# Score products that contract over their own 32 or 64 rows, in a two-block transformer kernel on one core

## The chip, the core and the metric

The kernel runs on one core of a Trainium2 chip. Five engines of the core work side by side, each through its own list of instructions in order: PE (TensorE, matrix products into PSUM banks), DVE (VectorE), ACT (ScalarE), POOL (GpSimd) and SP, which only issues DMAs. They wait for each other through semaphores. The metric is the device time of one execution in microseconds (us), the median of several runs.

A matmul loads a stationary operand (PEld in the profile) and streams the other through an array of 128 rows (the contraction) by 128 columns. A matmul whose operands occupy 32 or 64 partitions uses only that group of the array's rows; such a part is called a tile of the array below, written rows x columns (32x128, 64x128).

## What is computed

Two transformer blocks follow each other, each with two layers, on 256 tokens of width 1024. The first block mixes tokens with three branches (latent attention, differential attention, pooling), the second with sliding-window attention, an mLSTM and an RWKV-7 recurrence. Cut to the products that matter here:

```
# differential attention, 8 heads, two maps m of 32 channels each
sc = einsum('bqhmd,bkhmd->bmhqk', q, k) * scale - slopes * dist
a  = softmax(sc)[:, 0] - lam * softmax(sc)[:, 1]
# sliding-window attention, 8 query heads on 2 key heads of 64 channels
scores = einsum('bnqhgd,bnkhd->bnhgqk', qb, kb) * HEAD_DIM ** -0.5
# mLSTM, 4 heads of 64 channels
s = einsum('bhcld,bhcsd->bhcls', q, k) * w_intra
# RWKV-7, 4 heads of 64 channels, in the kernel's chunked form:
# products of (b, k) with (a, r) over the 64 channels of a head
```

## The kernel before

Activations lie transposed, channels on the 128 partitions and 256 tokens along the free dimension, so one 128-partition slab holds four 32-channel maps or two 64-channel heads. Large products run as fp32r pairs: each weight tile is split into a high part (`wh`, ACT, L444) and a low part (`wl`, DVE, L445), and `mm3` (L329) issues three fp32r matmuls per tile. The score products, transposes and recurrences are plain fp32, and each plain fp32 matmul appears in the trace as two MATMUL rows of its size, two passes.

In the plain form a score product contracts over all 128 partitions. To get one head out of the slab, one operand is first multiplied with a 0/1 column (`m4` or `m2`) that clears the other heads' rows:

- differential attention (`diff` in `_mix_a`, L1047 to L1055): four masked copies `qm` of the query slab on DVE for each slab and query half `qt`; for each head two matmuls (maps m = 0, 1) into one bank `S`; one DVE instruction adds the distance term for both maps. The score is 256 keys wide for `qt` = 1 and 128 for `qt` = 0.
- RWKV (`rwkv`, L1230 to L1278): two masked copies `BKm` of `BK` (DVE and ACT); for each of eight units (half `h`, slab `j`, head `e`) two 256-wide matmuls into one bank `rw`, then a DVE mask.
- mLSTM (`mlstm`, L1464 to L1493): two masked query copies on ACT; for each head a 256-wide and a 128-wide matmul into `S`.
- sliding window (`swa`, L1559 to L1579): two masked key copies on DVE; for each of four query slabs and each `qt` two matmuls into one bank `S`.

PSUM banks come from pools with a fixed number of buffers: `mm` 2 (also used by the projections), `S` 2 in the first block's mixer and 1 in the second's, `rw` 2, `PT` and `O`. The mixers are generators whose parts are written alternately with the projections of `gemm` (in the second block RWKV alternates with mLSTM and then the window attention). The final order on each engine is chosen by the framework's list scheduler when the kernel is built; only instructions passed to `chain` or `behind` are held in place. None of the score products is.

Of the kernel before, what the change touches and what calls it, by code (L numbers as in the profile page):

```python
# [13 lines left out]
AF = mybir.ActivationFunctionType  # L14
ALU = mybir.AluOpType
# [3 lines left out]
P = 128  # L19
T = 256  # L20
# [5 lines left out]
NEG = -1e30  # L26
# [186 lines left out]
def two(b):  # L213
    return b.rearrange("p (a t) -> p a t", a=2)
# [6 lines left out]
def bc(x, n):  # L221

    return x.unsqueeze(1).to_broadcast([x.shape[0], n, x.shape[1]])
# [641 lines left out]
def _mix_a(s, nrm, l, nxt, ws, ahead):  # L865
    nc, A = s.nc, s.A
# [21 lines left out]
    rq, _ = s.rstd(s.colsum(sq1), 2, 256 / 96, 96 * EPS)  # L888
    sq2 = s.tile([P, T], "row")
    nc.scalar.activation(sq2, ckv, AF.Square)  # L890
    rk, _ = s.rstd(s.colsum(sq2), 2, P)
# [3 lines left out]
    for j in range(2):  # L895
        b = s.gemm([A["a_win"][l, 7]], act)[0] if j else bp
# [6 lines left out]
    for c in range(3):  # L903
        b = s.ps("S")
# [28 lines left out]
    for c in range(2):  # L933
        b = s.ps("S")
# [8 lines left out]
    for h in range(2):  # L943
        b = s.ps("S")
# [10 lines left out]
    for st in range(4):  # L955
# [4 lines left out]
        m = s.tile([P, T], "row")  # L960
# [5 lines left out]
    for c in range(2):  # L966
        b = s.ps("S")
        for j in range(2):
            g = 2 * c + j
            s.mm3(b[:, j * T:(j + 1) * T], wp, g * P, P, pq[g], j == 0, True)  # L970
        for j in range(2):
            g = 2 * c + j
            y = s.tile([P, T], "row")
            nc.vector.tensor_scalar(y, b[:, j * T:(j + 1) * T], s.v(f"a_pb_{l}", g), s.v(f"a_ps_{l}", g),
                                    op0=ALU.add, op1=ALU.mult)
            s.split(yp[g][:, 0], yp[g][:, 1], y)

    dqk = Wide(s, 8, "cc")
# [61 lines left out]
    def diff(qt):  # L1040
        nk = P * (qt + 1)
        ob = s.ps("O")
        dm = s.dist[:, 0:256] if qt else s.dist[:, 256:384]
        for j in range(4):
            qm = s.tile([P, 4, P], "qm")
            for i in range(4):
                nc.vector.tensor_scalar(qm[:, i], dqk[j][:, qt * P:(qt + 1) * P], s.c("m4", i, i + 1), None, op0=ALU.mult)  # L1047
            for e in range(2):
                hd = 2 * j + e
                b = s.ps("S")  # L1050
                for m in range(2):
                    nc.tensor.matmul(b[:, m * nk:(m + 1) * nk], lhsT=qm[:, 2 * e + m], rhs=dqk[4 + j][:, :nk],
                                     start=True, stop=True)
                sc = s.tile([P, 2, nk], "sc")
                nc.vector.scalar_tensor_tensor(sc, bc(dm, 2), -(2.0 ** -(hd + 1)), two(b[:, :2 * nk]), op0=ALU.mult, op1=ALU.add)  # L1055
                rs = softmax_rows(s, sc)
# [7 lines left out]
                if hd == 7:  # L1064
# [12 lines left out]
                    for i in range(2):  # L1077
                        hi, lo = yd.pair(i)
# [62 lines left out]
def rwkv(s, nrm, l, rb, first, wrk, yh, yl):  # L1141
# [87 lines left out]
    nc.vector.tensor_tensor(BK[:, 1], k2, Ei, op=ALU.mult)  # L1229
    BKm = [s.tile([P, 2, 2, T], "ra") for _ in range(2)]  # L1230
    nc.vector.tensor_scalar(BKm[0], BK, s.c("m2", 0, 1), None, op0=ALU.mult)
    nc.scalar.activation(BKm[1], BK, AF.Copy, scale=s.c("m2", 1, 2))
    shift(0, b0)
# [33 lines left out]
    un = []  # L1267
    for h in range(2):
        for j in range(2):
            for e in range(2):  # L1270
                u = 4 * h + 2 * j + e
                b = s.ps("rw")
                rhs = AR[:, 2 * j + h].rearrange("p a t -> p (a t)")
                nc.tensor.matmul(b[:, 0:T], lhsT=BKm[e][:, 1, j, hs(h)], rhs=rhs, start=True, stop=True)
                nc.tensor.matmul(b[:, T:], lhsT=BKm[e][:, 0, j, hs(h)], rhs=rhs, start=True, stop=True)
                if u % 2 == 0:
                    un.append(s.tile([P, 2, 512], "ra"))
                nc.vector.tensor_tensor(un[u // 2][:, u % 2], b, s.m("mk4"), op=ALU.mult)  # L1278
            yield
# [136 lines left out]
def mlstm(s, nrm, l, rb, wif, yh, yl):  # L1416
# [32 lines left out]
    for c in range(2):  # L1449
# [13 lines left out]
        yield  # L1463
    qm = s.tile([P, 2, 2, T], "att")  # L1464
    for e in range(2):
        nc.scalar.activation(qm[:, e], qk[:, 0:2], AF.Copy, scale=s.c("m2", e, e + 1))
    va = s.tile([P, 2, 4, 65], "va")
# [13 lines left out]
    for hd in range(4):  # L1481
        j, e = hd // 2, hd % 2
        bm = s.ps("PT")
        nc.tensor.matmul(bm[:, :T], lhsT=s.c("ident")[:4, hd:hd + 1].to_broadcast([4, P]), rhs=M[:4], start=True, stop=True)
# [4 lines left out]
        nc.scalar.activation(wm[:, T:], wm[:, T:], AF.Exp, bias=cm[:, 4 + hd:5 + hd])  # L1489
        b = s.ps("S")  # L1490
        nc.tensor.matmul(b[:, :T], lhsT=qk[:, 2 + j, :P], rhs=qm[:, e, j], start=True, stop=True)
        nc.tensor.matmul(b[:, T:T + P], lhsT=qk[:, 2 + j, P:], rhs=qm[:, e, j, P:], start=True, stop=True)
        nc.vector.scalar_tensor_tensor(wm, b[:, :384], 1.0 / 32, wm, op0=ALU.mult, op1=ALU.mult)  # L1493
        if e == 0:
# [39 lines left out]
def swa(s, nrm, l, rb, yh, yl):  # L1534
# [23 lines left out]
    rope(kv[:, 0:1], 1)  # L1558
    km = s.t2("km")  # L1559
    for e in range(2):  # L1560
        nc.vector.tensor_scalar(km[:, e], kv[:, 0], s.c("m2", e, e + 1), None, op0=ALU.mult)
    yield
# [6 lines left out]
    for qt in (1, 0):  # L1569
        nk = P * (qt + 1)  # L1570
        ob = s.ps("O")
        for i in range(4):
            b = s.ps("S")
            for e in range(2):
                nc.tensor.matmul(b[:, e * nk:(e + 1) * nk], lhsT=q[:, i, qt * P:(qt + 1) * P], rhs=km[:, e, :nk],  # L1575
                                 start=True, stop=True)
            sc = s.tile([P, 2, nk], "sc")
            nc.vector.scalar_tensor_tensor(sc, bc(s.m("sw", 0 if qt else P, 256), 2), NEG, two(b[:, :2 * nk]),
                                           op0=ALU.mult, op1=ALU.add)  # L1579
            mx, sm, es, rs = (s.tile([P, 2], "t8") for _ in range(4))  # L1580
# [214 lines left out]
```

## Time and profile before

| | |
|---|---|
| median of 3 runs | 2460.52 us (2458.12 to 2463.18) |
| profiled execution: its time, its span | 2463.42 us, 2461.6 us |
| PE busy | 2400.8 us (98% of the span) |
| DVE, ACT, POOL busy | 1854.3, 1476.0, 43.6 us |
| mean granted TensorE clock | 0.992 of full |

The mixers of the first block lie at about 241 to 395 and 846 to 1000 us, those of the second at 1447 to 1600 and 2061 to 2215 us; the rest are feed-forward stages. A matmul's duration in the trace is a modelled latency that overlaps its neighbours', so what a matmul costs PE is read from the distance between starts, not from its duration.

### The profile page before, as it was taken

The numbers are of one execution on the slowest core, as the hardware profiler recorded it, in microseconds if no ns is written. First come the engines' busy times: TensorE is split into PE (matmuls) and PEld (weight loads), VectorE is DVE, ScalarE is ACT, GpSimd is POOL, SyncE is SP. The second block draws the span as 40 slices with busy tenths as digits, with TensorE's granted clock in tenths as the row PEclk, the third lists the DMA queues.
The fourth block names the chain that finished last, engine by engine and source line by source line (L and its number), as shares of the span: only waits on it lengthen the run. The fifth ranks groups of instructions, "written<-read, shape, count | busy, mean of one in ns | idle before, by whom it ended". The sixth has DMA issues, their size and how long they took to land. (4 is left out here: it accounts for less than half of the span.)

```text
span 2461.6 us, 45601 instructions
## 1 busy us (share of the span) xinstructions
PE 2400.8 (98%) x17164; PEld 2232.8 (91%) x17164; DVE 1854.3 (75%) x3620; ACT 1476.0 (60%) x2954; POOL 43.6 (2%) x43
## 2 busy tenths in 40 slices
PE   8999999999999999999999999999989999999998
PEld 6999999999899999999999888989989998898997
DVE  7667988767766888877786688777767678877765
ACT  6556765656655676566565564466666566346664
POOL 0000000000000000000000000000000000000000
PEclk9999999999999999999999999999999999999998
DMA  6554445555555444555555532146535553215651
GB/s 223 185 188 156 146 138 171 189 189 189 176 191 193 136 148 146 172 194 187 185 182 187 189 131 86 35 170 208 194 110 178 189 189 131 86 35 172 211 197 60
DMA packets 110510, 396.62 MB, mean 161 GB/s; under 512 B 12752, under 2 KB 13264, under 8 KB 110288
## 3 DMA queue, kind: packets, MB, share of 16 engines
q1 hardware_dynamic: 109008, 391.33, 47.5%
q8 instruction: 135, 2.21, 0.4%
q10 hardware_dynamic: 1280, 2.36, 0.3%
q14 instruction: 87, 0.71, 0.1%
HBM read 392.60 MB, written 1.05 MB: 160 GB/s over the span
## 5 line engine op out<-in xcount | busy, mean ns | idle before, releaser
L445 DVE TENSOR_TENSOR wl<-raw,wh 128x512 fp32r<-128x512 f32 (+1 forms) x1446 | 980.4, 686 | 266.8 <-ACT wh L444 246.9
L444 ACT ACTIVATE wh<-raw 128x512 fp32r<-128x512 f32 (+1 forms) x1446 | 895.7, 628 | 472.9 <-PE mm L329 118.4
L336 PE MATMUL mm<-act,wh 128*128 128x512 f32 x1728 | 614.0, 395 | 13.0 <-ACT wh L444 8.9
L337 PE MATMUL mm<-act,wl 128*128 128x256 f32 x1728 | 482.8, 280 | 0.7 <-DVE wl L445 0.7
L329 PE MATMUL acc<-h,wh 128*128 128x256 f32 x2560 | 457.0, 280 | 0.0
L329 PE MATMUL mm<-act,wh 128*128 128x256 f32 (+1 forms) x2176 | 420.7, 289 | 9.5 <-ACT act L447 3.4
L336 PEld LDWEIGHTS mm<-act,wh 128*128 128x128 f32 x1728 | 324.5, 188 | 85.4 <-ACT wh L444 9.1
L329 PEld LDWEIGHTS acc<-h,wh 128*128 128x128 f32 x2560 | 391.2, 188 | 4.0 <-ACT h L444 0.3
L329 PEld LDWEIGHTS mm<-act,wh 128*128 128x128 f32 (+1 forms) x2176 | 341.5, 190 | 15.8 <-ACT act L447 4.5
L329 PE MATMUL acc<-h,wl 128*128 128x256 f32 x1280 | 355.7, 279 | 0.0
L337 PEld LDWEIGHTS mm<-act,wl 128*128 128x128 f32 x1728 | 326.8, 189 | 1.8 <-DVE wl L445 1.2
L329 PE MATMUL mm<-act,wl 128*128 128x256 f32 x1088 | 310.8, 287 | 0.0
L336 PE MATMUL up<-act,wh 128*128 128x512 f32 x832 | 296.4, 394 | 0.1
L329 PEld LDWEIGHTS acc<-h,wl 128*128 128x128 f32 x1280 | 240.5, 188 | 0.3
L337 PE MATMUL up<-act,wl 128*128 128x256 f32 x832 | 232.6, 280 | 0.0
L329 PEld LDWEIGHTS mm<-act,wl 128*128 128x128 f32 x1088 | 206.4, 190 | 2.6 <-issue 1.8
L336 PEld LDWEIGHTS up<-act,wh 128*128 128x128 f32 x832 | 156.3, 188 | 34.3 <-DVE uu L344 0.5
L337 PEld LDWEIGHTS up<-act,wl 128*128 128x128 f32 x832 | 157.3, 189 | 0.4
L343 ACT ACTIVATE jn<-mm 128x256 f32<-128x256 f32 x216 | 80.1, 371 | 83.7 <-PE mm L337 83.6
L728 ACT ACTIVATE ga<-ga 128x512 f32<-128x512 f32 x88 | 55.1, 630 | 93.5 <-DVE ga L727 93.4
L344 DVE TENSOR_TENSOR ga<-mm,jn 128x256 f32<-128x256 f32 x112 | 46.9, 419 | 64.7 <-ACT jn L343 64.7
L336 PE MATMUL acc<-act,wh 128*128 128x512 f32 x256 | 92.9, 401 | 1.4 <-ACT wh L444 1.4
(506 smaller groups left out, 3233.7 us busy)
## 6 DMA issues: line engine op xcount, KB each, us to landing
raw<-a_wgate SPq DMA_DIRECT2D x88, 512.0 KB, 4.5
raw<-a_wup SPq DMA_DIRECT2D x88, 512.0 KB, 4.1
raw<-a_wdown SPq DMA_DIRECT2D x88, 512.0 KB, 4.3
raw<-b_wgate SPq DMA_DIRECT2D x88, 512.0 KB, 4.5
raw<-b_wup SPq DMA_DIRECT2D x88, 512.0 KB, 4.3
raw<-b_wdown SPq DMA_DIRECT2D x88, 512.0 KB, 4.5
raw<-a_win SPq DMA_DIRECT2D x80, 512.0 KB, 3.7
raw<-a_wbr SPq DMA_DIRECT2D x24, 512.0 KB, 3.7
```

The source lines that it names most:

```text
L329: pin(s.nc.tensor.matmul(out, lhsT=w[x], rhs=a[:, y], start=start and i == 0, stop=stop and i == 2, skip_group_check=True))
L336: s.nc.tensor.matmul(bank, lhsT=hi, rhs=a.rearrange("p a t -> p (a t)"), start=start, stop=False, skip_group_check=True)
L337: s.nc.tensor.matmul(bank[:, :T], lhsT=lo, rhs=a[:, 0], start=False, stop=stop, skip_group_check=True)
L343: s.nc.scalar.activation(t, b[:, T:], AF.Copy)
L344: s.nc.vector.tensor_tensor(out[:, i], b[:, :T], t, op=ALU.add)
L444: pin(nc.scalar.activation(hi, src, AF.Copy))
L445: pin(nc.vector.tensor_tensor(lo, src, hi.bitcast(F32), op=ALU.subtract))
L728: nc.scalar.activation(ga, ga, AF.Silu)
```

## The change

The masked copies go. Each score matmul takes as operands only the partitions of its own head (32 in `diff`, 64 elsewhere), and the matmuls of different row groups write different PSUM banks. The instruction that consumed one bank with both maps becomes two, one for each bank (`diff`, `swa`). In `rwkv` two banks are taken per (h, j), in `mlstm` both heads of a slab are computed at once into one bank of `S` and one of `mm`, and in `swa` likewise `S` and `mm`. The window keys are copied once by ACT where DVE wrote two masked copies.

```diff
         for j in range(4):
-            qm = s.tile([P, 4, P], "qm")
-            for i in range(4):
-                nc.vector.tensor_scalar(qm[:, i], dqk[j][:, qt * P:(qt + 1) * P], s.c("m4", i, i + 1), None, op0=ALU.mult)
             for e in range(2):
                 hd = 2 * j + e
-                b = s.ps("S")
+                sc = s.tile([P, 2, nk], "sc")
+                bm = [s.ps("S")[:, :nk] for _ in range(2)]
                 for m in range(2):
-                    nc.tensor.matmul(b[:, m * nk:(m + 1) * nk], lhsT=qm[:, 2 * e + m], rhs=dqk[4 + j][:, :nk],
-                                     start=True, stop=True)
-                sc = s.tile([P, 2, nk], "sc")
-                nc.vector.scalar_tensor_tensor(sc, bc(dm, 2), -(2.0 ** -(hd + 1)), two(b[:, :2 * nk]), op0=ALU.mult, op1=ALU.add)
+                    g = slice((2 * e + m) * 32, (2 * e + m) * 32 + 32)
+                    nc.tensor.matmul(bm[m], lhsT=dqk[j][g, qt * P:(qt + 1) * P], rhs=dqk[4 + j][g, :nk], start=True, stop=True)
+                for m in range(2):
+                    nc.vector.scalar_tensor_tensor(sc[:, m], dm, -(2.0 ** -(hd + 1)), bm[m], op0=ALU.mult, op1=ALU.add)
...
-    BKm = [s.tile([P, 2, 2, T], "ra") for _ in range(2)]
-    nc.vector.tensor_scalar(BKm[0], BK, s.c("m2", 0, 1), None, op0=ALU.mult)
-    nc.scalar.activation(BKm[1], BK, AF.Copy, scale=s.c("m2", 1, 2))
...
         for j in range(2):
+            bs = [s.ps("rw"), s.ps("rw")]
+            for i in range(2):
+                for e in range(2):
+                    g = slice(e * 64, e * 64 + 64)
+                    nc.tensor.matmul(bs[e][:, i * T:(i + 1) * T], lhsT=BK[g, 1 - i, j, hs(h)],
+                                     rhs=AR[g, 2 * j + h].rearrange("p a t -> p (a t)"), start=True, stop=True)
+            un.append(s.tile([P, 2, 512], "ra"))
             for e in range(2):
...
-                nc.vector.tensor_tensor(un[u // 2][:, u % 2], b, s.m("mk4"), op=ALU.mult)
+                nc.vector.tensor_tensor(un[-1][:, e], bs[e], s.m("mk4"), op=ALU.mult)
...
-    qm = s.tile([P, 2, 2, T], "att")
-    for e in range(2):
-        nc.scalar.activation(qm[:, e], qk[:, 0:2], AF.Copy, scale=s.c("m2", e, e + 1))
...
         j, e = hd // 2, hd % 2
+        if e == 0:
+            bs = [s.ps("S"), s.ps("mm")]
+            for lo, hi, k in ((0, T, 0), (T, 384, P)):
+                for i in range(2):
+                    g = slice(i * 64, i * 64 + 64)
+                    nc.tensor.matmul(bs[i][:, lo:hi], lhsT=qk[g, 2 + j, k:k + P], rhs=qk[g, j, k:], start=True, stop=True)
...
-    km = s.t2("km")
-    for e in range(2):
-        nc.vector.tensor_scalar(km[:, e], kv[:, 0], s.c("m2", e, e + 1), None, op0=ALU.mult)
+    km = s.tile([P, T], "km")
+    nc.scalar.activation(km, kv[:, 0], AF.Copy)
...
-            b = s.ps("S")
+            bs = [s.ps("S")[:, :nk], s.ps("mm")[:, :nk]]
             for e in range(2):
-                nc.tensor.matmul(b[:, e * nk:(e + 1) * nk], lhsT=q[:, i, qt * P:(qt + 1) * P], rhs=km[:, e, :nk],
-                                 start=True, stop=True)
+                g = slice(e * 64, e * 64 + 64)
+                nc.tensor.matmul(bs[e], lhsT=q[g, i, qt * P:(qt + 1) * P], rhs=km[g, :nk], start=True, stop=True)
```

What this does to the order on PE, at three places. First the differential attention, first layer, `qt` = 1: a row gives the line, the operation, the output tile, the operands and the output's size. Before, at the two heads of one slab:

```order
L329 MATMUL mm_805_3774<-act_532_2420,wl_804_3771 128x256
L1052 MATMUL S_808_3831<-cc_677_3206,qm_807_3826 128x256 x2
L1052 MATMUL S_815_3853<-cc_677_3206,qm_807_3826 128x256 x2
L329 MATMUL mm_832_3895<-act_527_2376,wh_824_3879 128x256 x2
L329 MATMUL mm_832_3895<-act_527_2376,wl_825_3880 128x256
```

And after, at one head of the same attention:

```order
L1051 MATMUL S_844_3969<-cc_677_3206,cc_639_3014 128x256
L329 MATMUL mm_861_4012<-act_527_2376,wl_856_4001 128x256
L329 MATMUL mm_861_4012<-act_527_2376,wh_855_4000 128x256 x2
L329 MATMUL mm_861_4012<-act_527_2376,wl_856_4001 128x256
L1060 MATMUL O_779_3704<-cc_704_3331,pT_815_3845 128x64 x2
L1051 MATMUL S_845_3970<-cc_677_3206,cc_639_3014 128x256
L329 MATMUL mm_861_4012<-act_532_2420,wh_857_4004 128x256 x2
```

The two maps of a head, which stood in one run of four, now stand apart, with full 128-row matmuls between them.

Second, the stretch in the second block where the RWKV scores (`rw`) and the mLSTM scores (`S`, `mm`) are made, first layer. Before (L1274 and L1275 are RWKV, L1491 and L1492 mLSTM, L329 a projection):

```order
L1274 MATMUL rw_3902_18657<-rp_3863_18468,ra_3865_18474 128x256
L1275 MATMUL rw_3902_18657<-rp_3863_18468,ra_3865_18474 128x256
L329 MATMUL mm_3964_18887<-act_3770_17900,wh_3960_18879 128x256 x2
L1491 MATMUL S_3908_18674<-att_3871_18493,att_3814_18199 128x256
L1492 MATMUL S_3908_18674<-att_3871_18493,att_3814_18199 128x128
L329 MATMUL mm_3964_18887<-act_3770_17900,wl_3961_18880 128x256
```

After (L1269 is RWKV, L1480 mLSTM, L1482 spreads one row of 4 over the partitions, L1492 is the product with the values):

```order
L1269 MATMUL rw_3915_18634<-rp_3879_18452,ra_3880_18453 128x256 x2
L1482 MATMUL PT_3927_18671<-row_3820_18144,cst_4_63 128x256
L1480 MATMUL S_3919_18644<-att_3830_18183 128x256
L1480 MATMUL mm_3920_18645<-att_3830_18183 128x256
L1480 MATMUL S_3919_18644<-att_3830_18183 128x128
L1480 MATMUL mm_3920_18645<-att_3830_18183 128x128
L1480 MATMUL mm_3933_18693<-att_3830_18183 128x256
L1480 MATMUL mm_3933_18693<-att_3830_18183 128x128
L1269 MATMUL rw_3916_18635<-rp_3879_18452,ra_3880_18453 128x256 x2
L1482 MATMUL PT_3934_18698<-row_3820_18144,cst_4_63 128x256
L1269 MATMUL rw_3924_18662<-rp_3879_18452,ra_3880_18453 128x256 x2
L1492 MATMUL O_3923_18658<-va_3885_18473,sc_3922_18652 128x65
```

The RWKV scores now come bank by bank, both matmuls of a bank (one row group) together, and the projection's rows between them have moved behind this stretch.

Third, the window attention of the same layer, after (L1570 is the score product, `S` for the lower and `mm` for the upper 64 rows; L1308 and L1313 belong to RWKV); before, each slab's two matmuls stood as one row with x2:

```order
L1570 MATMUL mm_4034_19188<-km_3983_18926,att_3986_18940 128x256
L1299 MATMUL rw_3985_18934<-ra_3945_18744,ra_3931_18689 128x128 x2
L1299 MATMUL rw_3985_18934<-ra_3945_18744,ra_3939_18716 128x128 x2
L1308 MATMUL rw_4000_19017<-ra_3946_18745,ra_3944_18743 128x128 x4
L1570 MATMUL S_4033_19187<-km_3983_18926,att_3986_18940 128x256
L1313 MATMUL rw_4001_19023<-ra_3944_18743,ra_3946_18745 128x128 x4
L1570 MATMUL mm_4045_19233<-km_3983_18926,att_3986_18940 128x256
L1570 MATMUL mm_4058_19290<-km_3983_18926,att_3986_18940 128x256
```

Here too the two row groups of a slab are separated by full matmuls, and two matmuls of the same row group can stand together.

## Rows read from the trace of the kernel before

**Rows 1.** The page, part 1: busy us of each engine (share of span).

```profile
PE 2400.8 (98%) x17164; PEld 2232.8 (91%) x17164; DVE 1854.3 (75%) x3620; ACT 1476.0 (60%) x2954; POOL 43.6 (2%) x43
```

**Rows 2.** Stretches: window, length, busy us of PE, PEld, DVE, ACT, POOL; clock, DMA.

```profile
241.00:395.00 154.00, 154.00 (x1259) 149.20 (x1258) 134.16 (x330) 102.94 (x250) 3.81 (x2) 1.00 0.46 147
1447.00:1600.00 153.00, 148.63 (x1153) 137.59 (x1152) 121.04 (x293) 70.71 (x160) 7.37 (x4) 0.99 0.21 72
```

**Rows 3.** Waits of PE, 1447 to 1600 us: total us, times, longest.

```profile
PE mm L372 <- DVE sc L1452: 1.2, 1, 1.2
PE rw L1217 <- DVE ud L1212: 1.2, 1, 1.2
PE mm L329 <- ACT va L1471: 1.0, 1, 1.0
PE PT L1443 <- DVE row L1437: 0.5, 1, 0.5
PE mm L329 <- DVE att L1566: 0.3, 1, 0.3
```

**Rows 4.** Groups by form, score matmuls: busy us, mean ns, idle before.

```profile
L1052 PE MATMUL S<-cc,qm 128*128 128x256 f32 x64 | 15.6, 382 | 0.0
L1274 PE MATMUL rw<-rp,ra 128*128 128x256 f32 x32 | 9.5, 379 | 0.0
L1575 PE MATMUL S<-km,att 128*128 128x256 f32 x32 | 8.2, 380 | 0.0
L1491 PE MATMUL S<-att,att 128*128 128x256 f32 x16 | 5.1, 399 | 0.0
```

**Rows 5.** Timeline of PE: start us, us, engine, line; 128-row tiles.

```profile
1539.25 1.03 PE L1575 MATMUL S<-km,att 128*128 128x256 f32 x4
1540.12 1.05 PE L1318 MATMUL rw<-ra,ra 128*128 128x128 f32 x8
1541.01 0.64 PE L1304 MATMUL rw<-ra,ra 128*128 128x128 f32 x4
```

**Rows 6.** Timeline of PE: a 64-row tile between 128-row tiles.

```profile
1526.00 0.94 PE L1304 MATMUL rw<-ra,ra 128*128 128x128 f32 x7
1526.87 0.71 PE L1388 MATMUL st<-rp,rp 64*128 64x128 f32 x4
1527.51 1.16 PE L1313 MATMUL rw<-ra,ra 128*128 128x128 f32 x8
1528.51 0.38 PE L1544 MATMUL PT<-sc,cst 128*128 128x256 f32 x1
```

**Rows 7.** Timeline of PE: a 4-row matmul (32-row tile) between projections.

```profile
1496.83 0.40 PE L329 MATMUL mm<-act,wh 128*128 128x256 f32 x2
1497.07 0.28 PE L329 MATMUL mm<-act,wl 128*128 128x256 f32 x1
1497.28 0.69 PE L1484 MATMUL PT<-row,cst 4*128 4x256 f32 x2
1497.90 0.50 PE L329 MATMUL mm<-act,wh 128*128 128x256 f32 x2
1498.24 0.28 PE L329 MATMUL mm<-act,wl 128*128 128x256 f32 x1
```

**Rows 8.** Timeline of PE: matmuls alternating between two 64-column tiles.

```profile
1564.34 1.09 PE L1333 MATMUL rw<-ra,rp 128*64 128x128 f32 x16
1565.37 0.49 PE L1575 MATMUL S<-km,att 128*128 128x128 f32 x2
```

**Rows 9.** Groups by form on DVE: busy us, mean ns, idle before.

```profile
L1047 DVE TENSOR_SCALAR qm<-cc,cst 128x128 f32<-128x128 f32 x64 | 14.0, 279 | 0.0
L1055 DVE SCALAR_TENSOR_TENSOR sc<-dist,S 128x512 f32<-128x512 f32 x16 | 10.9, 680 | 1.2 <-PE PT L844 0.9 <-PE S L1052 0.4
L1055 DVE SCALAR_TENSOR_TENSOR sc<-dist,S 128x256 f32<-128x256 f32 x16 | 6.6, 414 | 0.9 <-PE S L1052 0.7
L1231 DVE TENSOR_SCALAR ra<-ra,cst 128x1024 f32<-128x1024 f32 x2 | 1.5, 745 | 0.0
```

More of the change, by code (lines that the diff above doesn't have):

```diff
@@ L1269, in rwkv @@
         for j in range(2):
-            for e in range(2):
[L1271 to L1277, printed above, removed]
-                nc.vector.tensor_tensor(un[u // 2][:, u % 2], b, s.m("mk4"), op=ALU.mult)
+            bs = [s.ps("rw"), s.ps("rw")]
[5 more added lines that the diff above has]
+            un.append(s.tile([P, 2, 512], "ra"))
+            for e in range(2):
+                nc.vector.tensor_tensor(un[-1][:, e], bs[e], s.m("mk4"), op=ALU.mult)
             yield
@@ L1489, in mlstm @@
         nc.scalar.activation(wm[:, T:], wm[:, T:], AF.Exp, bias=cm[:, 4 + hd:5 + hd])
-        b = s.ps("S")
-        nc.tensor.matmul(b[:, :T], lhsT=qk[:, 2 + j, :P], rhs=qm[:, e, j], start=True, stop=True)
-        nc.tensor.matmul(b[:, T:T + P], lhsT=qk[:, 2 + j, P:], rhs=qm[:, e, j, P:], start=True, stop=True)
-        nc.vector.scalar_tensor_tensor(wm, b[:, :384], 1.0 / 32, wm, op0=ALU.mult, op1=ALU.mult)
+        nc.vector.scalar_tensor_tensor(wm, bs[e][:, :384], 1.0 / 32, wm, op0=ALU.mult, op1=ALU.mult)
         if e == 0:
@@ L1572, in swa @@
         for i in range(4):
-            b = s.ps("S")
+            bs = [s.ps("S")[:, :nk], s.ps("mm")[:, :nk]]
             for e in range(2):
-                nc.tensor.matmul(b[:, e * nk:(e + 1) * nk], lhsT=q[:, i, qt * P:(qt + 1) * P], rhs=km[:, e, :nk],
-                                 start=True, stop=True)
+                g = slice(e * 64, e * 64 + 64)
+                nc.tensor.matmul(bs[e], lhsT=q[g, i, qt * P:(qt + 1) * P], rhs=km[g, :nk], start=True, stop=True)
             sc = s.tile([P, 2, nk], "sc")
-            nc.vector.scalar_tensor_tensor(sc, bc(s.m("sw", 0 if qt else P, 256), 2), NEG, two(b[:, :2 * nk]),
-                                           op0=ALU.mult, op1=ALU.add)
+            for e in range(2):
+                nc.vector.scalar_tensor_tensor(sc[:, e], s.m("sw", 0 if qt else P, 256), NEG, bs[e], op0=ALU.mult, op1=ALU.add)
             mx, sm, es, rs = (s.tile([P, 2], "t8") for _ in range(4))
```

## The prediction

> **What bounds the kernel now.** I read the page's engine line first: PE is busy 98% of the span, the next engine (DVE) 75% [rows 1]. That is an average, so the second view is the two kinds of stretch that the change touches. In the first block's mixer PE is busy all of its 154 us while DVE has 20 us free; in the second block's, PE is busy 148.6 of 153 us and DVE 121 [rows 2]. The second layer's stretches read the same. So PE's own work sets the time in all four, and the waits that interrupt it are short: 4.2 us in a second-block stretch, the longest 1.2 us, for DVE or ACT [rows 3]. What the change is worth is therefore what it does to PE's list, plus what it does to those waits.
>
> A matmul's duration is a modelled latency (382 ns for L1052) [rows 4], and neighbours overlap it. What PE spends is the distance between starts. Four 256-wide plain fp32 passes take 1540.12 - 1539.25 = 0.87 us, 0.2175 each; eight 128-wide ones 0.89 us, 0.111 each [rows 5]. Each matmul is two passes: the 32 products that `diff` writes for 256 keys are 64 rows [rows 4]. So a 256-wide score matmul costs 0.435 us of PE and a 128-wide one 0.222.
>
> **What the change does on PE, part by part.**
>
> *The number of matmuls is the same.* By the code there are 88 score matmuls 256 wide (32 in `diff`, 32 RWKV, 16 window, 8 mLSTM; the groups of [rows 4] are twice that) and 56 128-wide (32, 16 and 8). They cost 88 x 0.435 + 56 x 0.222 = 50.7 us. Fewer rows of the array do not shorten a pass: L1388 contracts over 64 rows, and its four 128-wide passes need 0.64 us, not less than four full ones at 0.111 [rows 6]; L1484 contracts over 4 rows and needs 0.62 us for two passes 256 wide [rows 7].
>
> *What it can give: overlap.* No row of before has two row groups at work together. The nearest is L1333, which alternates between two groups of 64 columns: 16 passes of 128 columns take 1565.37 - 1564.34 = 1.03 us, where 16 alone would take 1.78 [rows 8]. Less about 0.1 us for leaving that shape (below), it is eight pairs at 0.11: full overlap. I take the same for row groups, and zero as the other bound. But overlap needs the two row groups next to each other on PE, and nothing holds them there. I went through the built order and counted. `diff`: only 4 of its 16 pairs with 256 keys stand together and 14 of 16 with 128. Window: 1 of 4 and 2 of 4 in each layer. RWKV: its matmuls come two by two, but of one bank and thus one row group, so none of its own pairs overlap; beside mLSTM's, in each layer two runs have a 256-wide and a 128-wide matmul under the other row group's. The gain is
>
> - `diff` 4 x 0.435 + 14 x 0.222 = 4.85 us,
> - window 2 x 0.435 + 4 x 0.222 = 1.76 us,
> - mLSTM and RWKV 4 x 0.657 = 2.63 us,
>
> 9.2 us in all, of 25.4 that overlap of every pair would give.
>
> *What it costs: changes of the tile's shape.* [Rows 6] show one round trip from 128 rows to 64 and back. Seven passes of L1304 before it take 0.87 us instead of 0.78 (+0.09); L1388 takes 0.64 instead of 0.44 (+0.20); the eight passes of L1313 behind it 1.00 instead of 0.89 (+0.11). Together 0.40 us. [Rows 7] show the same for a 32-row tile among fp32r projections: the last L329 0.21 instead of 0.12, L1484 0.62 instead of 0.435, the two L329 behind 0.34 instead of 0.24: 0.375 us. So each change of shape costs about 0.195 us, half of it before the switch (the array runs empty) and half behind (the first weights load with nothing over them). Neighbours of one shape, as in [rows 5], pay nothing. Along PE's built order the shape changes 112 times before and 263 times after; either bound of the round trip makes the 151 new ones 28.3 to 30.2 us, and I take 151 x 0.195 = 29.4 us. Most single score matmuls now bring a round trip of 0.39 us to work of 0.435.
>
> The Trainium skill, page "TensorEngine Tiling (Array Packing)", section "Key Properties", says that changing the tiling mode drains the engine, and gives no price. The rows show the drain (0.09) and as much again for the exposed load. By the drain alone the sum would be 151 x 0.09 - 9.2 = +4.4 us, about 2465; by the rows it is +20.2.
>
> *DVE and ACT.* The copies of L1047 (14.0 us busy) and L1231 (1.5) go [rows 9]. Two instructions for two banks cost more than one: 2 x 414 - 680 = 148 ns for each of 24 wide ones, and about 2 x 279 - 414 = 144 ns for each of 24 narrow ones (L1047's width stands in for the half) [rows 9], 7.0 us together. DVE is relieved by some 8.5 us, ACT by a few. In the first block this hides behind a PE without gaps [rows 2] and is worth nothing. In the second it could shorten waits for DVE and ACT, at most all of them, 2 x 4.2 = 8.4 us [rows 3]. But L1212, L1437 and L1452 stand ahead of the removed copies in the code, so I count zero and keep -8.4 as the bound.
>
> *Cover lost.* In the stretch of the RWKV and mLSTM scores, projections stood between the products. Now both `mm` banks hold mLSTM scores there, so the next projection has to wait until DVE has read one, and its rows have moved behind. What PE meets instead is L1482 and L1492, which wait for DVE and ACT, with RWKV's products queued behind them. A wait of the kind is 0.3 to 1.2 us [rows 3]. Bounds: none, since RWKV's matmuls still fill much of it, and one of 1.2 for each of four heads and two layers, 9.6 us. I take one of 1.0 per layer, 2 us, nearer the low end because the shape changes there already give DVE time.
>
> **Sum.** -9.2 + 29.4 + 2 = +22 us. On the profiled execution (2463.4, with a span of 2461.6) that is 2485.6. That execution lies 2.9 us above the median of the three runs, 2460.5, which spread over 5 us; on the median the sum is 2482.7. I give 2483, 0.9% slower. A measurement of this kernel can tell about 0.2%, 5 us, from no change.
>
> **Rivals.**
>
> 1. *Row groups don't overlap.* For it: no row shows it, and the column groups of [rows 8] read all 128 rows. Against it: banks and partitions are separate. Then the 9.2 us are not there: +31.4, 2492.
> 2. *Cover lost in full*: +9.6 instead of +2, 2490. For it the order's third and fourth heads, which wait on DVE; against it that PE, being later, finds more of its inputs ready.
> 3. *DVE's relief removes PE's waits*: +20.2 - 8.4 = +11.8, 2472. Against it the place of the copies.
> 4. *A switch costs the drain alone*, the load being hidden: +4.4, 2465. [Rows 6, 7] speak against it twice.
> 5. *Faster: switches are free*, because the 151 new ones fall where PE would wait or the engine prepares the next shape meanwhile. Place: every isolated score matmul. The change breaks even at 9.2 / 151 = 0.061 us a switch and is measurably faster below 0.03; at zero it is 2451. For it: RWKV and mLSTM products do stand near PE's waits [rows 3]. Against it: 0.19 us in both round trips, one of them among the projections that now surround `diff`. The Trainium skill, "TensorE: Matmul & The Clock Gate", "Part 3: Packing small matmuls", goes further and advises row slices because they run concurrently (3.07 times for four). As a mechanism here, all pairs overlapping without a price would be -25.4 us, 2435; the order rules that out for RWKV, whose pairs share a row group.
>
> **How the numbers follow.** The forecast, +14 to +27 us, gets 0.72; rival 1 0.10, rival 2 0.06, rival 3 0.05, rival 4 0.03 (no change that can be told), rival 5 0.04. The range runs from rival 3 (2472, less one us) to rival 1 with the profiled execution's 2.9 us and some lost cover (2496). Faster by over 0.2% is rival 5 alone, 0.04; within 0.2% rival 4, 0.03; slower the rest, 0.93.
>
> **What would show each step.** Switches: an isolated L1051 with 256 keys should start 0.21 us after the L329 ahead of it, hold PE for about 0.62 us, and the next L329 pair should need 0.34. Overlap: where S and `mm`, or two `S` banks, stand together, the second's start should follow the first's within some 10 ns and the run of four passes take about 0.65 us, switch in included, not 1.0. RWKV's two matmuls of a bank should still take 0.87 us plus the switch. Cover: new PE waits for DVE or ACT at L1482 and L1492. DVE's busy time should fall by about 8 us and change nothing. The forecast is wrong if PE's starts around single score products keep their old distances, or if the feed-forward stages, which the change leaves alone, move as well.

## The result and the profile after

The kernel after takes 2490.66 us (median of 4 runs, 2488.05 to 2494.63), the kernel before 2461.85 (4 runs, 2458.12 to 2464.73): a ratio of 1.0108, 95% interval 1.0090 to 1.0126. It is slower, as forecast (2483, 2471 to 2496), by 28.8 us where 22 were forecast. The profiled execution took 2494.63 us, with a span of 2492.8 us and a mean granted clock of 0.986.

The page of the kernel after, part 1, answers to [rows 1]:

```profile
PE 2433.0 (98%) x17164; PEld 2235.7 (90%) x17164; DVE 1847.7 (74%) x3598; ACT 1474.9 (59%) x2950; POOL 43.4 (2%) x43
```

PE has the same number of matmuls and is busy 32 us longer (part of that is the clock, as the experiments below tell). DVE is relieved by 6.6 us, with 22 instructions fewer, and nothing comes of it: PE remains the bound. The price of the second instruction is the one forecast. By the groups of DVE by form, which answer to [rows 9], two narrow ones cost 2 x 416 - 680 = 152 and 2 x 281 - 414 = 148 ns more than the one that they replace:

```profile
L1053 DVE SCALAR_TENSOR_TENSOR sc<-dist,S 128x256 f32<-128x256 f32 x32 | 13.2, 416 | 4.9 <-PE S L1051 4.8
L1053 DVE SCALAR_TENSOR_TENSOR sc<-dist,S 128x128 f32<-128x128 f32 x32 | 8.1, 281 | 2.4 <-PE S L1051 1.5 <-PE PT L844 0.9
```

The timeline of PE (start us, us, line, tile) shows the two mechanisms that the forecast rests on, first in `diff`, then among mLSTM's scores:

```profile
301.07 0.27 PE L844 MATMUL PT<-cst,sc 128*128 128x128 f32 x1
301.27 0.69 PE L1051 MATMUL S<-cc,cc 32*128 32x256 f32 x2
301.89 0.33 PE L844 MATMUL PT<-cst,sc 128*128 128x128 f32 x1
302.16 0.69 PE L1051 MATMUL S<-cc,cc 32*128 32x256 f32 x2
302.78 0.39 PE L329 MATMUL mm<-act,wh 128*128 128x256 f32 x1
...
1502.37 0.69 PE L1482 MATMUL PT<-row,cst 4*128 4x256 f32 x2
1502.99 0.48 PE L1480 MATMUL S<-att 64*128 64x256 f32 x1
1503.00 0.48 PE L1480 MATMUL mm<-att 64*128 64x256 f32 x1
1503.31 0.38 PE L1480 MATMUL S<-att 64*128 64x256 f32 x1
1503.32 0.38 PE L1480 MATMUL mm<-att 64*128 64x256 f32 x1
1503.53 0.27 PE L1480 MATMUL S<-att 64*128 64x128 f32 x1
...
1504.41 1.03 PE L1269 MATMUL rw<-rp,ra 64*128 64x256 f32 x4
1505.37 0.48 PE L1482 MATMUL PT<-row,cst 4*128 4x256 f32 x1
```

A lone L1051 holds PE for 301.89 - 301.27 = 0.62 us where a full one held it for 0.435 [rows 5], and the 128-row product ahead of it ends its turn 0.09 late (0.20 instead of 0.11): both halves of the forecast price. Where the two row groups stand next to each other (S and `mm` at 1502.99), they start within 0.01 us, and two products 256 wide pass in 1503.53 - 1502.99 = 0.54 us, 0.10 of it for the change of shape. RWKV's four passes at 1504.41 are of one row group and do not overlap: 0.96 us, 0.87 for the passes and 0.09 for the change behind them.

The stretches of the kernel after (window, length, busy us of PE, PEld, DVE, ACT, POOL; granted clock, DMA share, GB/s) hold what the forecast did not have. The first two answer to [rows 2], the others go through the RWKV and mLSTM scores of the first layer, and the last lies behind those of the second:

```profile
241.00:400.00 159.00, 159.00 (x1247) 146.24 (x1246) 130.84 (x313) 102.26 (x248) 3.80 (x2) 1.00 0.44 141
1458.00:1620.00 162.00, 157.79 (x1128) 139.35 (x1129) 119.28 (x296) 67.78 (x155) 7.37 (x4) 0.93 0.20 68
1493.00:1500.00 7.00, 6.35 (x45) 5.79 (x45) 7.00 (x16) 3.53 (x7) 0.00 (x0) 1.00 0.36 124
1500.00:1507.50 7.50, 7.50 (x43) 5.41 (x43) 7.50 (x18) 4.65 (x10) 0.00 (x0) 1.00 0.44 164
1507.50:1512.00 4.50, 4.50 (x20) 3.29 (x19) 1.50 (x3) 0.80 (x3) 0.00 (x0) 0.55 0.02 4
1512.00:1520.00 8.00, 8.00 (x24) 5.47 (x23) 2.40 (x5) 1.43 (x3) 0.00 (x0) 0.50 0.00 0
1520.00:1531.00 11.00, 11.00 (x40) 8.98 (x40) 5.46 (x14) 1.65 (x3) 0.00 (x0) 0.50 0.00 1
1531.00:1540.00 9.00, 9.00 (x76) 9.00 (x75) 5.16 (x14) 5.07 (x10) 1.64 (x1) 0.95 0.32 118
2132.60:2142.90 10.30, 10.30 (x34) 7.32 (x33) 3.02 (x6) 1.82 (x4) 0.00 (x0) 0.50 0.00 0
```

For 23.5 us PE runs at the lower of its two levels, 1.2 GHz, and loses 0.45 x 4.5 + 0.5 x 19 = 11.5 us of work there. It was never idle in the 7.5 us ahead of the fall; from 1501.31 on it ran short products of 64 and 4 rows with changes of shape between them. The second layer has the same products in the same order and a shorter fall, 10.3 us from 2132.6. And PE's waits in the stretch (total us, times, longest), which answer to [rows 3], are the old ones (L1149's stood just ahead of the window of [rows 3], with 1.6 us); none is at L1480, L1482 or L1492, in either layer:

```profile
PE mm L329 <- DVE ud L1149: 1.9, 1, 1.9
PE mm L372 <- DVE sc L1447: 1.2, 1, 1.2
PE rw L1215 <- DVE ud L1210: 1.2, 1, 1.2
PE mm L329 <- ACT va L1463: 1.0, 1, 1.0
PE PT L1438 <- DVE row L1432: 0.5, 1, 0.5
```

### The profile page after: what moved, and what is told of

Read it like the earlier page. It is cut to its first block, busy times and chain, and to the rows that moved or that the text cites. A ratio compares the mean times of both kernels' runs of the same rounds, so it can differ in the third digit from the quotient of the medians.

```text
span 2492.8 us, 45561 instructions
## 1 busy us (share of the span) xinstructions
PE 2433.0 (98%) x17164; PEld 2235.7 (90%) x17164; DVE 1847.7 (74%) x3598; ACT 1474.9 (59%) x2950; POOL 43.4 (2%) x43
## 5 line engine op out<-in xcount | busy, mean ns | idle before, releaser
L336 PE MATMUL mm<-act,wh 128*128 128x512 f32 x1728 | 614.5, 396 | 12.1 <-ACT wh L444 8.7
L329 PE MATMUL acc<-h,wh 128*128 128x256 f32 x2560 | 457.0, 280 | 0.0
L329 PE MATMUL mm<-act,wh 128*128 128x256 f32 (+1 forms) x2176 | 421.9, 290 | 8.7 <-ACT act L447 3.4
L329 PEld LDWEIGHTS acc<-h,wh 128*128 128x128 f32 x2560 | 391.1, 188 | 4.1 <-ACT h L444 0.3
L329 PEld LDWEIGHTS mm<-act,wh 128*128 128x128 f32 (+1 forms) x2176 | 343.5, 191 | 23.0 <-issue 11.9
L329 PE MATMUL acc<-h,wl 128*128 128x256 f32 x1280 | 355.7, 279 | 0.0
L329 PE MATMUL mm<-act,wl 128*128 128x256 f32 x1088 | 313.5, 289 | 0.0
L329 PEld LDWEIGHTS acc<-h,wl 128*128 128x128 f32 x1280 | 240.5, 188 | 0.3
L329 PEld LDWEIGHTS mm<-act,wl 128*128 128x128 f32 x1088 | 208.1, 191 | 4.0 <-issue 3.3
```

The costliest lines, as they stand in the source:

```text
L329: pin(s.nc.tensor.matmul(out, lhsT=w[x], rhs=a[:, y], start=start and i == 0, stop=stop and i == 2, skip_group_check=True))
L336: s.nc.tensor.matmul(bank, lhsT=hi, rhs=a.rearrange("p a t -> p (a t)"), start=start, stop=False, skip_group_check=True)
```

## The experiments

The theory going in: the loss is the counted changes of shape less the counted overlap (+20.2 us), and behind that the clock, which falls in the stretch of the RWKV and mLSTM scores. The rivals: the clock is something else's doing, or the count is right only by accident.

One figure is needed to read the runs. A mean clock of 0.986 over 2492.8 us means 2 x 0.014 x 2492.8 = 70 us at half clock, and 0.992 over 2461.6 us 39. It varies from one execution of the same kernel to the next, and the time with it: before took 2459.68 us at 0.993 and 2472.2 at 0.988. Over 134 executions of the kernels of this study, each measured against the mean of its own kernel, one slope fits: 1.81 us (95%: 1.62 to 1.99) for each 0.001 of clock, with 1.7 us of scatter left. The table's column "at equal clock" is a kernel's mean less the mean of before's 58 executions (2465.1 us at 0.9912), with that slope taken out; it is known to within about 1 to 2 us if the slope holds, and 0.195 us for each change of shape is not fitted in it.

That one slope serves every kernel is assumed. Half-clock time in which PE also waits costs less than half-clock time in a dense stretch: in the last 12 us of the kernel after, at half clock, PE is busy 3.3 us, in the 23.5 us above all of them. So the last column is a second reading, without the slope: PE's busy time in the profiled execution, less half of its busy time at half clock (that half is the work lost), against the same of before. For it, all stretches at half clock added up, the kernel after first, then before:

```profile
sum 69.90, PE 57.67 PEld 45.19 DVE 34.18 ACT 20.08 POOL 1.39; mean PE 8.24 PEld 6.46 DVE 4.88 ACT 2.87 POOL 0.20
sum 39.80, PE 28.47 PEld 25.19 DVE 26.29 ACT 16.02 POOL 1.40; mean PE 4.75 PEld 4.20 DVE 4.38 ACT 2.67 POOL 0.23
```

PE lost 28.8 and 14.2 us of work there, which leaves it 2404.2 and 2386.6 us of work at the full clock, 17.6 more than before. It is one execution of each kernel. Changes of shape are counted without 36 that every kernel has alike, at fp32r matmuls 32 and 64 columns wide.

| kernel | changes of shape | the count says | median less before's | mean clock | at equal clock | PE's work at full clock, profiled |
|---|---|---|---|---|---|---|
| after | 263 | +20.2 | +28.8 | 0.9868 | +17.9 | +17.6 |
| 1, `diff` only | 203 | +12.9 | +15.4 | 0.9900 | +12.1 | +13.2 |
| 2, second block only | 172 | +7.3 | +14.3 | 0.9865 | +5.2 | +4.9 |
| 9, RWKV only | 148 | +7.5 | +13.7 | 0.9877 | +7.3 | +6.0 |
| 7, mLSTM only | 118 | -0.1 | -2.3 | 0.9916 | -1.1 | +0.1 |
| 3, all pairs held | 228 | +0.9 | +5.9 | 0.9894 | +1.8 | +1.2 |
| 4, RWKV, mLSTM held | 132 | -3.9 | +1.2 | 0.9893 | -3.1 | -2.6 |
| 8, and `diff` on 64 rows | 172 | -5.4 | -1.0 | 0.9903 | -2.0 | -6.8 |
| 10, small rows made full | 88 | -4.7 | -10.9 | 0.9946 | -4.7 | +0.2 |
| 11, state products too | 68 | -8.6 | -12.9 | 0.9928 | -8.1 | -2.4 |

Before has 112 changes of shape. By both readings the kernel after and the seven partial or held ones lie near their count, within 3.4 and 2.6 us; for kernels 10 and 11 the two readings differ.

**The price of a change of shape, by itself (5 and 6).** The same added matmuls, once over 128 rows and once over 32 (shown).

```diff
+            if not last and o in (2, 6):
+                nc.tensor.matmul(acc[o // 2][:, :P], lhsT=s.zf[:32].to_broadcast([32, P]), rhs=s.c("ident")[:32], start=False, stop=False, skip_group_check=True)
```

> The kernel before, with 320 added matmuls in its feed-forward stages (four per group of down projections, 128 wide, of zero weights, so that they add nothing), that contract over 128 rows like their neighbours. They change no shape: 320 x 0.222 = +71 us, about 2535, under every theory. The control for the next kernel.

> The same 320 added matmuls at the same places, but over 32 of the rows: the only difference is 640 more changes of the tile's shape. Theory (0.195 us each): 640 x 0.195 = +125 us over the kernel with 128 rows, about 2660. Rival (the drain alone, 0.09): +58, 2593. Rival (switches are free and something else slowed the kernel after): the same time as with 128 rows. If shape changes bring the clock down, half-clock stretches appear in the feed-forward stages.

2525.48 us with 128 rows, 2650.46 with 32: 125.0 us for 640 changes, **0.195 us each**, the value that the forecast took from [rows 6, 7]. The drain alone (+58) and free switches (0) are out. The control itself missed: it came out 60.6 us above before and not 71, 0.19 us for a matmul; the price is the difference of the two kernels and does not rest on that. The mean clock is 0.994 in both, higher than before's. The timeline of PE with 32 rows shows one of them: 0.41 us for two passes that take 0.22 at full shape, 0.21 for the L331 ahead, 0.34 for the two behind.

```profile
82.64 0.39 PE L331 MATMUL acc<-h,wh 128*128 128x256 f32 x2
82.86 0.28 PE L331 MATMUL acc<-h,wl 128*128 128x256 f32 x1
83.07 0.48 PE L705 MATMUL acc<-cst,zf 32*128 32x128 f32 x2
83.48 0.50 PE L331 MATMUL acc<-h,wh 128*128 128x256 f32 x2
83.82 0.28 PE L331 MATMUL acc<-h,wl 128*128 128x256 f32 x1
```

The Trainium skill, "TensorEngine Tiling (Array Packing)", section "Key Properties", says that changing the mode, not just the tile, drains the engine. Both halves hold here: another row group of the same shape starts 0.01 us later, another shape costs 0.195, of which the drain is about half.

**The parts of the change apart (1, 2, 7, 9).** Each takes one function, or the second block's three, from the kernel after and leaves the rest as before; its edit is what the change's diff shows of that function.

> Only diff's scores are changed (tiles of 32 rows in two S banks); RWKV, mLSTM and the window attention are as before. Theory (each change of shape costs 0.195 us, each pair that stands together gives its overlap): 203 changes of shape instead of 112 are +17.7 us, overlap that the built order allows -4.85, so +12.9 us, about 2475, with the granted clock of the second block's stretches as before. Rival (whatever lies beyond the count in the whole change, some 11 us on 20, belongs to the narrow tiles wherever they are): 1.5 times that, +20, 2481. Rival (split banks and extra DVE instructions cost, not shapes): the isolated score matmuls keep their old start distances.

> RWKV, mLSTM and the window attention are changed, diff is as before. By the count 172 changes of shape instead of 112, +11.7 us, less 4.4 of overlap: +7.3, about 2469. Theory (the rest of the whole change's loss is the granted clock, which falls to half in the stretch of the RWKV and mLSTM scores): another 10 us, +17, about 2479, with some 20 to 30 us more at half clock than before. Rival (the clock fell because of the whole program's load, not of this stretch): +7, and the records show no half-clock stretch at these scores.

> Only mLSTM's scores are changed (both banks, S and mm, for a pair of heads), the rest is as before. By the count 118 changes of shape instead of 112 and 1.3 us more overlap: -0.1 us, the same as before. Rival (both mm banks are taken, so that the projections that stood between the scores move, and with that the clock falls, or PE waits): 5 to 10 us slower, with a mean granted clock near 0.987.

> Only RWKV's scores are changed, not held; diff, mLSTM and window as before. By the count 148 changes of shape instead of 112 (+7.0 us) and 0.4 us less overlap: +7.5. Theory (RWKV's products of 64 rows, which do not overlap because a bank's two share a row group, are what brings the clock down in that stretch): a mean granted clock near 0.987 and another 7 to 9 us, +15, about 2479. Rival (the clock falls only where RWKV's and mLSTM's narrow products meet): +7.5, about 2472, at a clock of 0.991 as before.

Measured: 2479.96 us (ratio 1.0059, 1.0045 to 1.0073), 2478.86 (1.0054, 1.0039 to 1.0069), 2462.52 (0.9999, 0.9987 to 1.0012) and 2479.42 (1.0048, 1.0034 to 1.0063). At equal clock the first three are within 2.1 us of the count, and RWKV within 0.2. `diff` costs what its changes of shape cost, with little from the clock; mLSTM alone costs nothing and leaves the clock alone, so that taking both `mm` banks does no harm. RWKV alone has both terms, +7.3 and 6.2 us of clock: the rival that the clock falls only where RWKV's and mLSTM's narrow products meet is out. But it does not fall every time: of its four executions three have 0.986 or 0.987 and take 2477.61 us or more, one has 0.991, like before, and takes 2474.34. The stretches of RWKV alone show the fall (the clock is the last number but two):

```profile
1486.00:1495.50 9.50, 9.50 (x55) 7.27 (x53) 5.75 (x11) 4.02 (x8) 0.00 (x0) 1.00 0.32 112
1495.50:1519.50 24.00, 24.00 (x76) 17.88 (x75) 8.84 (x18) 3.66 (x8) 0.00 (x0) 0.50 0.06 22
```

and its timeline of PE what stood ahead of it:

```profile
1492.31 1.13 PE L1271 MATMUL rw<-rp,ra 64*128 64x256 f32 x4
1493.37 0.39 PE L329 MATMUL mm<-act,wh 128*128 128x256 f32 x1
1493.68 1.13 PE L1271 MATMUL rw<-rp,ra 64*128 64x256 f32 x4
1494.74 0.39 PE L329 MATMUL mm<-act,wl 128*128 128x256 f32 x1
1495.06 0.69 PE L1481 MATMUL PT<-row,cst 4*128 4x256 f32 x2
```

Five short turns, six changes of shape, and no wait.

Kernel 2's profiled execution shows that the products alone do not decide it. Its two layers run the same RWKV and mLSTM products in the same order; the first layer's pass at the full clock, the second layer's fall to half for 23.9 us, with half as many matmuls done in the time:

```profile
1489.00:1513.00 24.00, 24.00 (x161) 19.93 (x160) 16.76 (x40) 9.84 (x20) 1.64 (x1) 1.00 0.19 67
2113.50:2137.40 23.90, 23.90 (x81) 18.09 (x81) 9.25 (x21) 3.53 (x8) 0.00 (x0) 0.50 0.00 0
```

**Pairs held together (3, 4, 8).** The matmuls of a group also wait for the last reader of the banks they take, so that both row groups come up at once:

```diff
+    def after(s, i, k):
+        if k in s.read:
+            s.tc.add_manual_dep(i.ins, s.read[k].name, mybir.DependencyInfo(mybir.DependencyClass.Sync, mybir.DependencyReason.DATA), reason="after")
+        return i
...
-                    nc.tensor.matmul(bs[e][:, i * T:(i + 1) * T], lhsT=BK[g, 1 - i, j, hs(h)],
-                                     rhs=AR[g, 2 * j + h].rearrange("p a t -> p (a t)"), start=True, stop=True)
+                    s.after(nc.tensor.matmul(bs[e][:, i * T:(i + 1) * T], lhsT=BK[g, 1 - i, j, hs(h)],
+                                             rhs=AR[g, 2 * j + h].rearrange("p a t -> p (a t)"), start=True, stop=True), "r")
...
+            s.read["r"] = last.ins
```

The third of them gives `diff` back its masks and pairs its two heads instead of its two maps:

```diff
+            bs = [s.ps("S"), s.ps("S")]
+            for m in range(2):
+                for e in range(2):
+                    g = slice(e * 64, e * 64 + 64)
+                    s.after(nc.tensor.matmul(bs[e][:, m * nk:(m + 1) * nk], lhsT=qm[g, 2 * e + m], rhs=dqk[4 + j][g, :nk],
+                                             start=True, stop=True), "d")
```

> All four parts are changed as in the kernel after, and each group of score matmuls also waits for the last reader of the banks that it takes, so that the two row groups of a pair stand next to each other in PE's order. By the count 228 changes of shape instead of 263 and 34.1 us of overlap instead of 21.6: 19 us less than the kernel after, 0.9 more than before, 2462 if the clock is granted. Theory (overlap is real wherever two row groups stand together, and the clock falls only where narrow products stand without projections): 2462 to 2475, by how long the clock is at half. Rival (pairs do not overlap as counted, or the new waits on DVE stop PE): 2490 or more.

> Only RWKV and mLSTM are changed, with their pairs held together as in the kernel that holds all; diff and the window attention are as before. By the count 132 changes of shape instead of 112 (+3.9 us) and 7.8 us more overlap: -3.9 us, about 2457, if the clock is granted. Theory (clock falls in the stretch of these scores): one stretch of each layer at half clock, 5 to 10 us, so 2460 to 2467. Rival (the clock has nothing to do with these products): 2457.

> RWKV and mLSTM as in the kernel that holds their pairs together; diff keeps its masks and its one bank and one DVE instruction per head, but the two heads of a column block contract over their own 64 rows, the four matmuls held together; the window attention as before. By the count 172 changes of shape instead of 112 (+11.7 us) and 17.1 us more overlap: -5.4 us, about 2459 against 2464.6 of before on that chip. Theory (count and clock): 2457 to 2463 by how often the clock falls. Rival (a pair's wait for both banks of S stops PE): slower than before.

In the expectation of kernel 3 the 21.6 and 34.1 us of overlap also hold 12.4 that before already has; the change's own are 9.2 and 21.7. Measured: 2470.54 us (1.0022, 1.0009 to 1.0036), 2465.77 (1.0001, 0.9989 to 1.0012) and 2463.84 (0.9993, 0.9981 to 1.0006). Holding the pairs of the kernel after leaves 5.9 us of its 28.8: overlap is real, and the kernel after gets only 9.2 us of it, by the count, because nothing holds its pairs together (held, there are also 35 changes of shape fewer, 6.8 us of the gain). No version of the idea is measurably faster than before. What the held pairs of RWKV and mLSTM gain (-3.1 at equal clock), the clock takes back (0.9893). Kernel 8 came out just above the 2457 to 2463 that were expected, and gained 3.4 us less than its count at equal clock. In its profiled execution PE's work is 6.8 us less, as much as the count says and more, while PE is idle 1.9 us longer and loses 13.1 us more to the clock, with 20.5 us at half clock in the second layer's stretch of these scores. Whether its other executions divide in the same way was not found.

**Runs of narrow matmuls by themselves (12).** In each of eight feed-forward stages, one run over 128 rows, one over 64, one over the two halves in turn:

```diff
+        for i in range(32 if j in (2, 5, 8) else 0):
+            e = i % 2 if j == 8 else 0
+            g = slice(0, P) if j == 2 else slice(e * 64, e * 64 + 64)
+            nc.tensor.matmul(acc[2 + e][:, :T], lhsT=s.zf[g].to_broadcast([P if j == 2 else 64, P]), rhs=s.cst[g, :T],
+                             start=False, stop=False, skip_group_check=True)
```

> The kernel before, with runs of 32 added matmuls (256 wide, of zero weights, so that they add nothing) in each of its eight feed-forward stages: behind the third group of down projections over 128 rows, behind the sixth over the same 64 rows, behind the ninth over the two halves of the rows in turn, in two banks. At full clock a run takes 13.9, 13.9 and 7.0 us, and each run of 64 rows brings two changes of shape. Theory (the clock falls behind products that use half the rows without a partner, not behind changes of shape): half-clock stretches begin in or just behind the second kind of run and not the first or third. Rival (the clock falls where PE works off the projections, whatever the rows): behind all three. Rival (it falls by chance, or by what DVE and ACT do): behind none. The third kind also measures overlap by itself: 7.0 us if pairs overlap, 13.9 if not.

2736.25 us in one run, mean clock 0.993. The stretches of the first three runs:

```profile
78.87:92.49 13.62, 13.62 (x66) 11.99 (x65) 0.76 (x2) 0.63 (x1) 0.00 (x0) 1.00 0.22 77
143.04:157.05 14.01, 14.01 (x65) 11.89 (x64) 0.69 (x1) 0.63 (x1) 0.00 (x0) 1.00 0.25 74
208.11:215.22 7.11, 7.11 (x66) 6.11 (x65) 2.46 (x4) 2.92 (x5) 0.00 (x0) 1.00 0.53 167
```

64 passes take 14.01 us in one row group and 7.11 in two: pairs overlap in full, and rows left out save nothing. The clock stays at 1.00 in all three, and in the 21 like them. So **the theory of the clock that this run was made for fell**: half the rows without a partner do not bring it down. These products have zero weights; data was not tried.

**The lesson turned round (10, 11).** Products that contracted over 4 or 32 rows before contract over 128, with zeros; then RWKV's state products too.

```diff
-    gi, gf, one = (s.tile([4, T], "row") for _ in range(3))
+    gz, Gz, Mz = (s.tile([P, T], "row") for _ in range(3))
+    for x in (gz, Gz, Mz):
+        nc.gpsimd.memset(x, 0.0)
...
-        nc.tensor.matmul(bm[:, :T], lhsT=s.c("ident")[:4, hd:hd + 1].to_broadcast([4, P]), rhs=M[:4], start=True, stop=True)
+        nc.tensor.matmul(bm[:, :T], lhsT=s.c("ident")[:, hd:hd + 1].to_broadcast([P, P]), rhs=Mz, start=True, stop=True)
```

In kernel 11 also, with `Kz` the halves of `Kt` and `Bt` among zeros:

```diff
-                nc.tensor.matmul(sb[:, o], lhsT=Kt[rs, h, o], rhs=Vt[rs, h, o], start=j == 0, stop=False, skip_group_check=True)
+                nc.tensor.matmul(sb[:, o], lhsT=Kz[:, c, o], rhs=Vt[:, h, o], start=j == 0, stop=False, skip_group_check=True)
...
-                ins = nc.tensor.matmul(sb[:, o], lhsT=Bt[rs, h, o], rhs=Us[rs, h, o], start=False, stop=True, skip_group_check=True)
+                ins = nc.tensor.matmul(sb[:, o], lhsT=Kz[:, 3, o] if c == 1 else Bt[:, h, o], rhs=Us[:, h, o], start=False, stop=True, skip_group_check=True)
```

> The lesson turned round: the score products stay as before, and products of before that contract over 4 or 32 rows (mLSTM's L1443 and L1484, diff's L1034) contract over 128, with rows of zeros, which the idle POOL writes. By the count 88 changes of shape instead of 112: 24 x 0.195 = -4.7 us, ratio 0.998. Rival (these changes of shape hide behind waits for DVE and ACT): no difference.

> As the last one, and RWKV's state products (L1388, L1391), which contract over 64 rows of tokens, contract over 128 with zeros in the other half of one operand; four ACT copies and two POOL memsets are added per layer. By the count 68 changes of shape instead of 112: 44 x 0.195 = -8.6 us, ratio 0.9965, about 2456 where before is 2464.6. Rival (the copies stand ahead of the state's chain, on which the last part of the stretch depends): up to 2 us lost per layer, -4.6.

2454.79 us (ratio 0.9953, 0.9941 to 0.9965) and 2452.81 (0.9952, 0.9937 to 0.9967): **both beat both kernels**. Both gain more than their counts (-4.7 and -8.6). At equal clock they give -4.7 and -8.1; the first also has the best clock of all. Its timeline of PE at the product of [rows 7]: from 1485.33 to 1486.12 three L329 and the two passes of L1488 take 0.79 us, 3 x 0.12 + 0.435, with nothing for a change of shape.

```profile
1485.33 0.40 PE L329 MATMUL mm<-act,wh 128*128 128x256 f32 x2
1485.57 0.59 PE L1488 MATMUL PT<-row,cst 128*128 128x256 f32 x2
1485.81 0.47 PE L329 MATMUL mm<-act,wl 128*128 128x256 f32 x1
1486.12 0.40 PE L329 MATMUL mm<-act,wh 128*128 128x256 f32 x2
```

By the slope, less than half of its 10.9 us is the shapes, and 6.2 go with the clock. The profiled executions, taken by themselves, divide it otherwise: of the 10.4 us between their spans 8.2 are work lost to the clock in before and not here, 2.5 are idle time of PE that is gone, and PE's work at the full clock is the same (+0.2). So the total is measured, and its division is not shown. Where the clock's part may come from: the waits of 1.2 us at L1217 and L372 [rows 3] are not in its first layer's stretch. Before has them behind a 4-row product, and the clock is 0.93 over the 25 us around them where this kernel has 1.00. The timeline of PE before:

```profile
1468.82 0.69 PE L1484 MATMUL PT<-row,cst 4*128 4x256 f32 x2
1470.73 1.16 PE L1217 MATMUL rw<-cst,ud 128*128 128x128 f32 x8 [1.22 <-DVE ud L1212]
1473.13 0.58 PE L372 MATMUL mm<-wh,act 128*128 128x256 f32 x1 [1.24 <-DVE sc L1452]
```

Its stretch around them (columns as above):

```profile
1460.00:1485.00 25.00, 21.45 (x158) 20.50 (x159) 23.46 (x50) 12.70 (x26) 3.35 (x1) 0.93 0.39 128
```

The same stretch of kernel 10:

```profile
1460.00:1485.00 25.00, 23.90 (x186) 22.52 (x186) 24.76 (x52) 14.78 (x26) 2.35 (x1) 1.00 0.52 168
```

That the clock follows the waits is inferred from these rows, and that the waits go because the new order brings DVE's work forward is a guess; neither was tried apart.

## Why the prediction was right, and where its size was off

- **Price of a pass, and no saving from fewer rows**: right. 14.01 us against 13.62 for 64 passes over 64 and 128 rows.
- **Overlap, -9.2 us**: right as a mechanism; the 9.2 themselves were counted and measured only as part of the sum. Pairs in two row groups overlap in full, those of one row group not at all, so rival 1 falls. That few pairs stand together was the built order's doing, as counted; held together they give the rest (kernel 3).
- **Changes of shape, +29.4 us**: right. 0.195 us each by kernels 5 and 6, and every partial or held kernel agrees with its count to 3.4 us at equal clock, and to 2.4 us by PE's work at the full clock. Rivals 4 and 5 fall.
- **DVE's relief, 0**: right in the main. DVE's busy time fell by 6.6 us for the 8.5 estimated (which left out the window's four masked key copies, 1.2 us), and PE's waits stayed, so rival 3 falls. The kernel after lies 2.3 us under its count at equal clock, known to about 2; at most some 4 us came of it.
- **"Cover lost" in the RWKV and mLSTM stretch, +2 us as new waits of PE at L1482 and L1492**: this step failed. No such wait is there. The place was right, but what PE lost there it lost to the clock, for which the prediction has no term and no rival: 4.4 thousandths of mean clock by 1.81 us are 8.0 us. In the first layer alone 11.5 us of work were lost in the profiled execution, behind 7.5 us in which PE never waited. Rival 2's time, 2490, is nearly what was measured, by a mechanism that the trace doesn't show; it is no hit.

The sum in its place: 17.9 us for shapes and overlap (20.2 by the count), 8.0 for the clock, 25.9 against all 58 executions of before; the four beside the result lay 3 us lower than those, which makes 28.8. The two profiled executions alone, 31.2 us apart, divide it as 17.6 of work and 14.6 of clock, less 1.0 of idle time; the one of the kernel after is the slowest of its four. So the clock's part is known less well, 8 to 15 us, than that of shapes and overlap, which comes out alike. The forecast held because its range reached up to 2496 for missing overlap and lost cover; that the clock fitted into that room is luck.

What stays open is what exactly brings the clock down. Shown: RWKV's row groups make it fall more often and longer (9), mLSTM's do not (7), 640 more changes of shape among projections do not (6), nor do long runs over half the rows (12). What is left is their mixture: short runs of narrow products, each between two changes of shape, with few projections between. The mixture does not settle it either: in kernel 2 the same list of products ran at the full clock in one layer and at half in the other, in the kernel after it fell for 23.5 us in one and 10.3 in the other, and one of kernel 9's four executions has the clock of before. The Trainium skill, "TensorE: Matmul & The Clock Gate", "Part 1: The HAM clock gate", says that the gate goes by how busy PE has lately been. The fall of before behind two waits agrees; in the kernel after the profile calls PE busy all through the 7.5 us ahead of the fall, so busy time in the profile is not what shows it.

## What to carry to other kernels

Count changes of the tile's shape along the built order of PE, not rows saved: here each cost 0.195 us, nearly as much as a plain fp32 pass 256 wide (0.2175), and narrow tiles pay only in a run in which matmuls of different row groups stand next to each other and whose overlap is worth more than its two changes. Where a small contraction stands alone among full ones, pad it with zeros to all rows, if an idle engine can write the zeros: that made this kernel 0.5% faster, by a division between shapes, waits and clock that was not shown. And when a dense stretch gets slower than the sum of its parts, look at the granted clock of the stretch before looking for a wait.

## What was unexpected of the hardware

The clock's share: one kernel's executions lay 12.5 us apart with mean clocks of 0.993 and 0.988, and 1.81 us for each 0.001 explains all but 1.7 us of scatter within each kernel. PE fell to half clock for 23.5 us behind 7.5 us in which it had never waited, and the same products in the same order ran at the full clock in one layer of kernel 2 and at half in the other. Two row groups in two banks start 0.01 us apart and give all of a factor of two (14.01 to 7.11 us).
